# A reordered opening: inputs and square sums first, filter products in pairs, k/v blocks of one k-tile

## The chip, the cores and the metric

The kernel runs on one core of a Trainium2 chip (trn2). The metric is the device time of one execution in microseconds (us); lower is better. A profile of one execution lies beside the times. Engines: TensorE (PE; its weight loads are PEld), VectorE (DVE), ScalarE (ACT), GpSimd (POOL) and SyncE (SP, which issues nearly all transfers).

## The reference

One layer of a hybrid diffusion block, in float32, for 256 latent tokens `x` and 256 context tokens `ctx`, width 2048:

```python
mod = (silu(c) @ ada_w + ada_b)          # six vectors: sh1, sc1, g1, sh2, sc2, g2
mod_c = silu(c_ctx) @ ada_w + ada_b
h  = rmsnorm(x,   norm1_g) * (1 + sc1)  + sh1
hc = rmsnorm(ctx, norm1_g) * (1 + csc1) + csh1
q, k, v, f, hy = split(h @ w_in)
kc, vc = split(hc @ w_in[:, 1024:3072])
```

Behind it stand neighbourhood attention over the latent and all context keys (8 heads of 128), a 2-D Fourier mix of `f`, and a Hyena operator on `hy`: long convolutions through FFTs, whose filters are made by a small network of positions: `hdn = sin(freq * (z @ w1 + b1))`, `hdn = sin(freq * (hdn @ w2 + b2))`, `h = (hdn @ w3) * decay`. Each group has its own RMSNorm, then come `w_out`, a gated residual, a gated MLP with a depthwise convolution (11 x 512 hidden columns), another gated residual and a final RMSNorm.

## The kernel before

Activations lie transposed, features on the 128 partitions, 16 "k-tiles" of 128 features by 256 tokens. Large products are made in three passes of reduced-precision fp32 (fp32r): each operand is split into a rounded part `hi` and a remainder `lo`, and `mm3` (line 163) adds hi*hi, hi*lo and lo*hi. A weight chunk of 1 MB comes in two transfers of 512 KB into buffers called `raw` (8 of them, line 238), ACT casts it to `w_hi` (line 172) and DVE subtracts for `w_lo` (line 173); two chunks of split weights can exist. Small products are plain f32 matmuls, each of which the profile shows as two instructions.

**The k/v projection** (k and v of x and ctx together, 2048 columns) is the first large stage. Its 16 k-tiles are worked in `blocks=(2, 2, 4, 4, 4)`. A block has four groups (`group`, line 511): two for k (`kT`, 256-column matmuls) and two for v (`v_t`, 512-column matmuls). Each group fills four of the five `acc_ps` PSUM banks, and each block's sums go to `kT` and `v_t`: block 0 by a copy on ACT (line 534), later blocks by an add on DVE (line 536). Before a block can run, its k-tiles need the adaLN scale and shift: `prep_pieces` (line 439) loads the block's columns of `ada_w` (4 MB for two k-tiles), multiplies them with the two silu vectors (line 454, tiles of 32 columns, four side by side), transposes and reduces; then `hprep` (line 483) makes hi and lo of h and hc, per k-tile and input two DVE operations (lines 224, 229) and one on ACT (line 228). While block b runs, the pieces of block b+1 are made. `CFG["p1"]` says how many side steps (`pump`: two columns of adaLN rows for later stages, two DVE operations of line 317 and 1 MB of transfers) come in each block.

**The opening** comes before that. `CFG["start"]` lists its steps by short names: transfers (`hp`, `pk` the packed constants, `h3` hy_w3, `dc` decay, `ft` the DFT table, `x0 x1` and `c0 c1` the inputs, `a..` adaLN columns), `si` the silu, `n1s n2s` the two sine layers, `hw` sums of hy_w3, `w0` to `w3` warm-up matmuls whose results nobody reads, `fr` first filter rows, `f0 f1` the filters of the two orders, `s0 s1` their spectra, `q0 q1` square sums and `n0 n1` the norms of x and ctx, `p0 p1` adaLN of block 0, `w` the first weight chunks, `h0 h1` hi and lo of block 0, `e` a piece of block 1. The filters `kz` have one buffer, so `f0 s0 f1 s1` follow each other.

The order in the list is not the order on an engine. The framework that builds the program (Tile) orders each engine's queue itself, with the list as priorities and a table of expected costs, and sets all waits. Within a queue the chip then keeps that order.

**Square sums before:** ACT squares 512 columns at a time, DVE reduces four such into one [128, 256] part (line 427, eight in all), PE sums over partitions with one-column matmuls, DVE and ACT take the reciprocal root of two columns, and `rms_bcast` (line 201) spreads it again by two diagonal matrices (`dg`, line 212) and two matmuls:

```python
for t in range(2):
    dg = cst.tile([P, P], F32, tag="dg", name="dg", bufs=2)
    TS(dg[:], ident, r[:, t : t + 1], None, op0=ALU.mult)
    mm(ps[:, t * P : (t + 1) * P], ones[:], dg[:], True, True)
```

Of the kernel before, what the change touches and what calls it, by code (L numbers as in the profile page):

```python
# [8 lines left out]
F32 = mybir.dt.float32  # L9
# [26 lines left out]
for _n, _k in V_LAYOUT:  # L36
# [10 lines left out]
    p1=(3, 0, 3, 5, 6),  # L47
    blocks=(2, 2, 4, 4, 4),
# [78 lines left out]
def hybrid_block(ctx: ExitStack, tc: tile.TileContext, a: dict, out: bass.AP):  # L127
# [103 lines left out]
    class Weights:  # L231
        def __init__(self, stack, nraw, nsp, side=None):
            self.raw = pool(stack, "w_raw", nraw, side)
            self.sp = pool(stack, "w_split", nsp, side)

# [5 lines left out]
        def chunk(self, src, i, nk, n):  # L241
            raws = []
            for q in range(2):
                z = (slice(None), slice(q * nk // 2, (q + 1) * nk // 2))
                raws.append((z, self.load(src[2 * i + q], nk // 2, n)))
# [35 lines left out]
    class Pairs:  # L281
# [5 lines left out]
        def add(self):  # L287
            self.tiles.append(self.pool.tile([P, 2, L], self.dt, tag=self.pool.name, name=self.name, bufs=KT // 2))
# [68 lines left out]
    if True:  # L357
        hpack = w1.raw.tile([64, L + 2 * 64 + 3], F32, tag="raw", name="hpack")
        hw3, hwsd = spec[:64, 0], spec[:64, 1]
# [5 lines left out]
        hw2 = hpack[:, 67:131]  # L365
        zT = hpack[:33, 131 : 131 + L]
        hd1, hd2 = tb[:64, 2, :L], tb[:64, 2, L:]
# [5 lines left out]
        def sine(dst, w, src, b):  # L373
            ps = bank()
            mm(ps[:64, :L], w, src, True, True)
            arg, k = tb[:64, 3, :L], tb[:64, 3, L:]
            TS(arg, ps[:64, :L], hv[:, b : b + 1], hv[:, 2:3], op0=ALU.add, op1=ALU.mult)
# [5 lines left out]
            nc.scalar.activation(dst, arg, AF.Sin)  # L383
# [13 lines left out]
        def first_row(o):  # L397
            ps = bank()
            mm(ps[0:1, :], hd2[:, 0:1], hw3[:, 2 * o, :], True, True)
            TT(frow[:, o, :], ps[0:1, :], decay[0:1, 0, :], op=ALU.mult)  # L400

        def filters(o):
            for t in range(2):
                for z in range(2):
                    ps = bank()
                    mm(ps[:], hd2[:, t::2], hwsd[:, 2 * o + z, :], True, True)
                    TT(kz[:, 2 * z + t, :], ps[:], decay[:, t, :], op=ALU.mult)
            for z in range(2):
                nc.scalar.copy(kz[0:1, 2 * z, :], frow[:, o, :])
# [5 lines left out]
    if True:  # L415
# [4 lines left out]
        def squares(v):  # L420
            parts = []
            for q in range(4):
                pt = v_t[:, q, v * L : (v + 1) * L]
                sq = kT[:, 2 * (q % 2) : 2 * (q % 2) + 2, :].rearrange("p a (b n) -> p a b n", n=L)
                for j in range(2):
                    nc.scalar.activation(sq[:, j], xs[v].tiles[2 * q + j][:], AF.Square)
                nc.vector.tensor_reduce(pt, sq.rearrange("p a b n -> p n (a b)"), axis=AX.X, op=ALU.add)
# [55 lines left out]
        def hprep(k0, nk, vv):  # L483
            ts = []
            for k in range(k0, k0 + nk):
                hi, lo = hs[vv]
                A, B = (z[:, k, vv : vv + 1] for z in (A1, B1))
                ts.append((modulate(p1, xs[vv][:, k, :], A, rbs[vv][:]), B, hi[:, k, :]))
                if k % 2:
                    lo.add()  # L490
                    for i in range(2):
                        t, B, h = ts[i]
                        shift_split(t, B, h, lo[:, k - 1 + i, :])
                    ts = []
# [16 lines left out]
        def group(b, g):  # L511
# [19 lines left out]
            for u in range(4):  # L531
                dst = kT[:, 4 * g + u, :] if g < 2 else v_t[:, u, (g - 2) * 512 : (g - 1) * 512]
                if b == 0:
                    nc.scalar.copy(dst, pss[u][:])
                else:
                    TT(dst, pss[u][:], dst, op=ALU.add)
# [9 lines left out]
        def first_rows():  # L546
            first_row(0)
            first_row(1)

        def sq(v):  # L550
            parts[v] = squares(v)

        wn = CFG["warm"]
        steps = {
            "hp": lambda: nc.sync.dma_start(hpack[:], a["hpack"]),
            "pk": lambda: nc.sync.dma_start(pack[:], a["pack"]),
            "h3": lambda: nc.sync.dma_start(hw3, a["hy_w3"][0].rearrange("k (g n) -> k g n", n=HYW)),
# [4 lines left out]
            "w0": lambda: warm(ones[:], wn[0]), "w1": lambda: warm(decay[:, 0, :], wn[1]),  # L562
            "w2": lambda: warm(ftab.rearrange("p a n -> p (a n)"), wn[2]), "w3": lambda: warm(xs[0][:, 0, :], wn[3]),
# [3 lines left out]
            "a00": lambda: pre_ada(0, 0), "a01": lambda: pre_ada(0, 1), "a10": lambda: pre_ada(1, 0), "a11": lambda: pre_ada(1, 1),  # L567
# [5 lines left out]
        late = CFG["late"].split()  # L573
        for z in CFG["start"].split():
            steps[z]()
        for b in range(len(blocks)):
# [3 lines left out]
            for g in range(4):  # L580
# [3 lines left out]
                while late and b == 0:  # L584
                    z = late.pop(0)
                    if z == "|":
                        break
                    steps[z]()
# [322 lines left out]
def laid_out(inp):  # L911
# [25 lines left out]
    h = np.zeros((64, L + 2 * 64 + 3), f32)  # L937
    for i, n in enumerate(("hy_b1", "hy_b2", "hy_freq")):
        h[:, i] = inp[n][0]
    h[:33, 3:67] = inp["hy_w1"][0]  # L940
    h[:, 67:131] = inp["hy_w2"][0]
    h[:33, 131:] = z.T
# [4 lines left out]
    def tiled(chunks, halves=2):  # L947
        out = np.empty((len(chunks) * halves, P, 1024), f32)
        for i, (w, k, nk, c, n) in enumerate(chunks):
            nk //= halves  # L950
            for q in range(halves):
                z = inp[w][0, (k + q * nk) * P : (k + (q + 1) * nk) * P, c : c + n]
                out[halves * i + q] = z.reshape(nk, P, n).transpose(1, 0, 2).reshape(P, nk * n)
        return out
# [35 lines left out]
```

## Time and profile before

| | |
|---|---|
| median of 3 runs | 1358.14 us (1357.56 to 1358.69) |
| the profiled execution | 1356.83 us, its span 1354.8 us, granted TensorE clock 0.988 |
| PE busy | 1319.2 us, 97% of the span |
| DVE, ACT busy | 921.9 us (68%), 553.0 us (41%) |
| read from memory | 308 MB, 229 GB/s over the span |

"Busy" for PE means that some matmul was in the pipeline. In a group's row the name says what is written from what, then partitions x elements, count, busy us, mean ns of one, and the idle time of the engine just before with what ended it. A mean can be longer than the distance between two starts, since matmuls overlap. In the chain of waits each line is a start, a length and what the end of the program hung on then. The window rows give busy us (and counts) per engine, then the granted clock, the busy share of the transfer engines and their rate.

### The profile page before, as it was taken

The numbers are of one execution on the slowest core, as the hardware profiler recorded it, in microseconds if no ns is written. First come the engines' busy times: TensorE is split into PE (matmuls) and PEld (weight loads), VectorE is DVE, ScalarE is ACT, GpSimd is POOL, SyncE is SP. The second block draws the span as 40 slices with busy tenths as digits, with TensorE's granted clock in tenths as the row PEclk, the third lists the DMA queues.
The fourth block names the chain that finished last, engine by engine and source line by source line (L and its number), as shares of the span: only waits on it lengthen the run. The fifth ranks groups of instructions, "written<-read, shape, count | busy, mean of one in ns | idle before, by whom it ended". The sixth has DMA issues, their size and how long they took to land.

```text
span 1354.8 us, 24555 instructions
## 1 busy us (share of the span) xinstructions
PE 1319.2 (97%) x10318; PEld 1237.8 (91%) x10318; DVE 921.9 (68%) x1200; ACT 553.0 (41%) x741; POOL 43.6 (3%) x32
## 2 busy tenths in 40 slices
PE   8899999999989999999999999999999999999996
PEld 4587888899879889989999999999999999999996
DVE  5856658687999888976676767744445555554553
ACT  3443213143333665445444444433334444443442
POOL 0000000000422010000000000000000000000000
PEclk9899999999989999989999999999999999999998
DMA  8788678697776964846777777755555555555541
GB/s 320 264 313 332 256 287 315 239 345 237 215 264 234 349 208 158 288 147 205 259 252 251 240 250 252 269 188 189 186 187 189 184 188 190 187 187 189 185 152 62
DMA packets 92894, 311.96 MB, mean 230 GB/s; under 512 B 15984, under 2 KB 16176, under 8 KB 92464
## 3 DMA queue, kind: packets, MB, share of 16 engines
q1 hardware_dynamic: 92784, 310.41, 66.4%
q8 instruction: 80, 1.31, 0.4%
q14 instruction: 30, 0.25, 0.0%
HBM read 308.27 MB, written 2.10 MB: 229 GB/s over the span
## 4 chain that ended last, share of the span: by engine, by line
PE 89%; DVE 6%; issue 2%; ACT 1%; DMA 1%; POOL 0%; DVEq 0%; ACTq 0%; POOLq 0%
PE acc_ps L161 82%; PE mi_ps L161 4%; PE mi_ps L454 2%; DVE w_lo L173 2%; DVE acc L317 1%; PE mi_ps L169 1%; DMA raw<-in_ada_t 1%; DMA raw<-in_ada_col_t 0%; DVE X L736 0%; DVE xr L906 0%; DVE u L654 0%; ACT w_hi L172 0%; DVE u L746 0%; DVE u L655 0%; DVE Y L729 0%
## 5 line engine op out<-in xcount | busy, mean ns | idle before, releaser
L173 DVE TENSOR_TENSOR w_lo<-raw,w_hi 128x1024 fp32r<-128x1024 f32 x376 | 453.5, 1236 | 234.7 <-ACT w_hi L172 233.4
L172 ACT CAST w_hi<-raw 128x1024 fp32r<-128x1024 f32 x376 | 380.3, 1048 | 515.3 <-PE acc_ps L161 452.0
L161 PE MATMUL acc_ps<-h_hi,w_hi 128*128 128x256 f32 x1408 | 395.5, 281 | 1.6 <-ACT h_hi L228 1.6
L161 PE MATMUL acc_ps<-h_hi,w_lo 128*128 128x256 f32 x1408 | 395.4, 281 | 0.0
L161 PE MATMUL acc_ps<-h_lo,w_hi 128*128 128x256 f32 x1408 | 395.4, 281 | 0.0
L161 PEld LDWEIGHTS acc_ps<-h_hi,w_hi 128*128 128x128 f32 x1408 | 266.1, 189 | 1.8 <-ACT h_hi L228 1.8
L161 PEld LDWEIGHTS acc_ps<-h_lo,w_hi 128*128 128x128 f32 x1408 | 266.1, 189 | 0.0
L161 PEld LDWEIGHTS acc_ps<-h_hi,w_lo 128*128 128x128 f32 x1408 | 266.1, 189 | 0.0
L161 PE MATMUL acc_ps<-yh,w_lo 128*128 128x256 f32 x704 | 197.1, 280 | 0.0
L161 PE MATMUL acc_ps<-yl,w_hi 128*128 128x256 f32 x704 | 197.1, 280 | 0.0
L161 PE MATMUL acc_ps<-yh,w_hi 128*128 128x256 f32 x704 | 196.8, 280 | 0.0
L317 DVE SCALAR_TENSOR_TENSOR acc<-raw,s_t,acc 128x1024 f32<-128x1024 f32 x120 | 160.6, 1338 | 32.6 <-DMA raw<-in_ada_col_t 31.8
L161 PE MATMUL acc_ps<-hx_hi,w_lo 128*128 128x256 f32 x512 | 146.1, 286 | 4.9 <-DVE w_lo L173 4.9
L161 PE MATMUL acc_ps<-hx_hi,w_hi 128*128 128x256 f32 x512 | 146.4, 286 | 0.0
L161 PE MATMUL acc_ps<-hx_lo,w_hi 128*128 128x256 f32 x512 | 145.0, 283 | 0.0
L161 PEld LDWEIGHTS acc_ps<-yl,w_hi 128*128 128x128 f32 x704 | 132.4, 188 | 0.0
L161 PEld LDWEIGHTS acc_ps<-yh,w_hi 128*128 128x128 f32 x704 | 132.2, 188 | 0.0
L161 PEld LDWEIGHTS acc_ps<-yh,w_lo 128*128 128x128 f32 x704 | 132.1, 188 | 0.0
L161 PEld LDWEIGHTS acc_ps<-hx_hi,w_lo 128*128 128x128 f32 x512 | 97.5, 191 | 7.6 <-DVE w_lo L173 5.5
L161 PEld LDWEIGHTS acc_ps<-hx_hi,w_hi 128*128 128x128 f32 x512 | 97.7, 191 | 4.3 <-issue 4.2
L161 PEld LDWEIGHTS acc_ps<-hx_lo,w_hi 128*128 128x128 f32 x512 | 97.6, 191 | 0.5 <-issue 0.4
L633 DVE SCALAR_TENSOR_TENSOR xr<-acc_ps,G,xr 128x256 f32<-128x256 f32 x64 | 26.9, 477 | 25.1 <-PE acc_ps L161 25.1
(225 smaller groups left out, 1595.2 us busy)
## 6 DMA issues: line engine op xcount, KB each, us to landing
raw<-in_ffn_t SPq DMA_DIRECT2D x264, 512.0 KB, 4.2
raw<-in_ada_col_t SPq DMA_DIRECT2D x128, 512.0 KB, 5.0
raw<-in_ada_t SPq DMA_DIRECT2D x64, 512.0 KB, 6.4
raw<-in_w_in_t SPq DMA_DIRECT2D x48, 512.0 KB, 5.6
raw<-in_w_kv_t SPq DMA_DIRECT2D x32, 512.0 KB, 5.2
raw<-in_w_out_t SPq DMA_DIRECT2D x32, 512.0 KB, 4.8
x_in<-in_xT SPq DMA_DIRECT2D x8, 256.0 KB, 7.3
x_in<-in_cT SPq DMA_DIRECT2D x8, 256.0 KB, 8.2
```

Of the source, the lines that this page charges most:

```text
L161: nc.tensor.matmul(ps, lhsT, rhs, start=start, stop=stop, skip_group_check=True)
L169: nc.tensor.transpose(ps, src, ident[:n, :n])
L172: nc.scalar.copy(hi, src)
L173: TT(lo, src, hi.bitcast(F32), op=ALU.subtract)
L317: STT(acc[:], r[:, 0, :], sc, acc[:], op0=ALU.mult, op1=ALU.add)
L454: nc.tensor.matmul(ps[32 * j : 32 * j + 32, :w], s_t[:, kt, :], raws[kt // (n2 // 2)][:, kt % (n2 // 2), :], start=kt < 4, stop=kt >= KT - ...
L633: STT(xr[:, c, :], pss[nt // 2][:, (nt % 2) * L : (nt % 2 + 1) * L], cols[:, c : c + 1], xr[:, c, :], op0=ALU.mult, op1=ALU.add)
```

## The change

1. **Order.** The list becomes the one in the diff. The two packs are issued from ACT, and SP starts with x and ctx, then hy_w3, decay, the DFT table, the adaLN columns of block 0 and, early, the first weight chunk (`W`). Warm-up: 8 matmuls on ones and 3 on `pack`; the 11 others go.
2. **Square sums.** PE multiplies the squared tiles with a matrix of ones, 16 matmuls of 256 columns per input, which leaves the sum on all partitions; `rms_rows` takes the reciprocal root on [128, 256] and no broadcast is needed.
3. **Filter products.** hy_w3 and hy_w2 are held twice, on partitions 0 to 63 and 64 to 127, so that two products of 64 rows lie on the two halves of the array and are issued next to each other into two banks.
4. **Blocks.** `blocks` becomes (1, 1, 2, 4, 4, 4), `p1` (0, 2, 1, 3, 5, 6). A chunk of one k-tile has 2048 columns and comes in two column halves; the host lays it out so. Block 0's v copies go to DVE. `hprep` makes one k-tile at a time, and the pool of pairs for `lo` gets one buffer more.

```diff
-    p1=(3, 0, 3, 5, 6),
-    blocks=(2, 2, 4, 4, 4),
+    p1=(0, 2, 1, 3, 5, 6),
+    blocks=(1, 1, 2, 4, 4, 4),
...
-    start='hp pk h3 dc ft x0 x1 si w0 n1s w1 n2s hw w2 w3 a00 a01 a10 fr q0 f0 p0 a11 p1 n0 h0 s0 c0 w c1 f1 e s1 q1 n1 h1 e',
-    late='',
-    warm=(8, 2, 6, 3),
+    start='hp pk x0 x1 c0 c1 h3 dc ft a0 a1 W wm si n1s wp n2s q0 q1 n0 hw n1 fr f0 s0 f1 p0 p1 w h0 h1 s1 e',
+    warm=(8, 3),
...
+    def rms_rows(pool_, ps, n, name):
+        ms = pool_.tile([P, L], F32, name=f"{name}_m", tag="rr_m")
+        TS(ms[:], ps[:, :L], 1.0 / n, EPS, op0=ALU.mult, op1=ALU.add)
+        s = pool_.tile([P, L], F32, name=f"{name}_s", tag="rr_s")
+        r = pool_.tile([P, L], F32, name=f"{name}_r", tag=f"{name}_r")
+        nc.scalar.activation(s[:], ms[:], AF.Sqrt)
+        nc.vector.reciprocal(r[:], s[:])
+        STT(s[:], r[:], -0.5, ms[:], op0=ALU.mult, op1=ALU.mult)
+        TT(s[:], s[:], r[:], op=ALU.mult)
+        STT(r[:], s[:], 1.5, r[:], op0=ALU.add, op1=ALU.mult)
+        return r
...
+                if nk > 1:
+                    z = (slice(None), slice(q * nk // 2, (q + 1) * nk // 2))
+                    raws.append((z, self.load(src[2 * i + q], nk // 2, n)))
+                else:
+                    z = (slice(None), slice(None), slice(q * n // 2, (q + 1) * n // 2))
+                    raws.append((z, self.load(src[2 * i + q], 1, n // 2)))
+            return raws
+
+        def load_early(self, src, i, nk, n):
+            self.early[id(src), i] = self.loads(src, i, nk, n)
...
-        hpack = w1.raw.tile([64, L + 2 * 64 + 3], F32, tag="raw", name="hpack")
-        hw3, hwsd = spec[:64, 0], spec[:64, 1]
+        hpack = w1.raw.tile([P, L + 3 * 64 + 3], F32, tag="raw", name="hpack")
+        hw3, hwsd = spec[:, 0], spec[:, 1]
...
+        def rows(o):
+            return slice(64 * o, 64 * o + 64)
...
         def filters(o):
             for t in range(2):
+                pss = [bank(acc_ps) for _ in range(2)]
                 for z in range(2):
-                    ps = bank()
-                    mm(ps[:], hd2[:, t::2], hwsd[:, 2 * o + z, :], True, True)
-                    TT(kz[:, 2 * z + t, :], ps[:], decay[:, t, :], op=ALU.mult)
+                    mm(pss[z][:], hd2[rows(z), t::2], hwsd[rows(z), 2 * o + z, :], True, True)
+                for z in range(2):
+                    TT(kz[:, 2 * z + t, :], pss[z][:], decay[:, t, :], op=ALU.mult)
...
         def squares(v):
-            parts = []
-            for q in range(4):
-                pt = v_t[:, q, v * L : (v + 1) * L]
-                sq = kT[:, 2 * (q % 2) : 2 * (q % 2) + 2, :].rearrange("p a (b n) -> p a b n", n=L)
-                for j in range(2):
-                    nc.scalar.activation(sq[:, j], xs[v].tiles[2 * q + j][:], AF.Square)
-                nc.vector.tensor_reduce(pt, sq.rearrange("p a b n -> p n (a b)"), axis=AX.X, op=ALU.add)
-                parts.append(pt)
-            return parts
-
-        def normalise(v, parts):
-            rbs[v] = rms_bcast(p1, parts, D, f"rs{v}")
+            ps = bank(acc_ps)
+            for q in range(KT // 2):
+                sq = kT[:, (q + 4 * v) % NH, :].rearrange("p (k n) -> p k n", n=L)
+                nc.scalar.activation(sq, xs[v].tiles[q][:], AF.Square)
+                for i in range(2):
+                    mm(ps[:, :L], ones[:], sq[:, i], q + i == 0, q == KT // 2 - 1 and i == 1)
+            return ps
+
+        def normalise(v, ps):
+            rbs[v] = rms_rows(p1, ps, D, f"rs{v}")
...
-                if b == 0:
+                if b == 0 and g < 2:
                     nc.scalar.copy(dst, pss[u][:])
+                elif b == 0:
+                    nc.vector.tensor_copy(dst, pss[u][:])
                 else:
                     TT(dst, pss[u][:], dst, op=ALU.add)
...
+        def load_w3():
+            for z in range(2):
+                nc.sync.dma_start(hw3[64 * z : 64 * z + 64], a["hy_w3"][0].rearrange("k (g n) -> k g n", n=HYW))
...
-            "hp": lambda: nc.sync.dma_start(hpack[:], a["hpack"]),
-            "pk": lambda: nc.sync.dma_start(pack[:], a["pack"]),
+            "hp": lambda: nc.scalar.dma_start(hpack[:], a["hpack"]),
+            "pk": lambda: nc.scalar.dma_start(pack[:], a["pack"]),
```

More of the change, by code (lines that the diff above doesn't have):

```diff
@@ L234, in __init__ @@
             self.sp = pool(stack, "w_split", nsp, side)
+            self.early = {}
         def load(self, src, nk, n):
@@ L364, in hybrid_block @@
         hw1 = hpack[:33, 3:67]
-        hw2 = hpack[:, 67:131]
-        zT = hpack[:33, 131 : 131 + L]
-        hd1, hd2 = tb[:64, 2, :L], tb[:64, 2, L:]
+        hw2 = hpack[:64, 67:195]
+        zT = hpack[:33, 195 : 195 + L]
+        hd1, hd2 = tb[:64, 2, :L], tb[:, 2, L:]
         def silu():
@@ L487, in hprep @@
                 A, B = (z[:, k, vv : vv + 1] for z in (A1, B1))
-                ts.append((modulate(p1, xs[vv][:, k, :], A, rbs[vv][:]), B, hi[:, k, :]))
-                if k % 2:
+                t = modulate(p1, xs[vv][:, k, :], A, rbs[vv][:])
+                if k % 2 == 0:
                     lo.add()
[L491 to L494, printed above, removed]
+                shift_split(t, B, hi[:, k, :], lo[:, k, :])
         w_specs, w_at = [], {}
@@ L561, in hybrid_block @@
             "si": silu, "n1s": lambda: sine(hd1, hw1, zT, 0), "n2s": lambda: sine(hd2, hw2, hd1, 1), "hw": sums,
-            "w0": lambda: warm(ones[:], wn[0]), "w1": lambda: warm(decay[:, 0, :], wn[1]),
-            "w2": lambda: warm(ftab.rearrange("p a n -> p (a n)"), wn[2]), "w3": lambda: warm(xs[0][:, 0, :], wn[3]),
+            "wm": lambda: warm(ones[:], wn[0]), "wp": lambda: warm(pack[:, :384], wn[1]), "W": lambda: w1.load_early(*w_specs[0]),
             "c0": lambda: load_pairs(xs[1], a["cT"], 0), "c1": lambda: load_pairs(xs[1], a["cT"], 1),
@@ L572, in hybrid_block @@
         }
-        late = CFG["late"].split()
         for z in CFG["start"].split():
@@ L583, in hybrid_block @@
                 group(b, g)
[L584 to L588, printed above, removed]
                 budget += CFG["p1"][b] / 4.0
```

48 lines of the change are left out of this document (24 added, 24 removed).

## The prediction

> **What bounds the kernel now.** I read the page first, then a table of the opening stretches, then the chain of waits, then the groups of the opening, keeping shapes apart. The page and its chain:
>
> ```profile
> span 1354.8 us, 24555 instructions
> PE 89%; DVE 6%; issue 2%; ACT 1%; DMA 1%; POOL 0%; DVEq 0%; ACTq 0%; POOLq 0%
> ```
>
> TensorE (PE) sets the time. Where does it not? The table by stretch (busy us of PE, PEld, DVE, ACT, POOL; then granted clock, DMA share, GB/s):
>
> ```profile
> 0.00:27.00 27.00, 22.11 (x54) 10.80 (x54) 18.09 (x27) 8.40 (x15) 0.90 (x7) 1.00 0.93 332
> 27.00:40.00 13.00, 6.96 (x87) 4.61 (x87) 6.87 (x20) 7.16 (x11) 0.00 (x0) 0.86 0.88 328
> 40.00:48.00 8.00, 7.66 (x18) 3.35 (x17) 7.96 (x13) 4.90 (x9) 0.00 (x0) 0.79 0.90 327
> 48.00:65.40 17.40, 17.25 (x135) 10.77 (x134) 14.78 (x30) 4.25 (x9) 0.00 (x0) 1.00 0.50 169
> 65.40:114.00 48.60, 48.59 (x323) 37.59 (x323) 28.78 (x55) 21.25 (x36) 0.00 (x0) 1.00 0.87 335
> 114.00:230.00 116.00, 116.00 (x760) 94.01 (x760) 79.01 (x126) 27.73 (x38) 0.00 (x0) 1.00 0.78 289
> ```
>
> From 65.4 to 230 us PE is never idle (48.59 of 48.60, 116 of 116), while VectorE (DVE) works 59% and 68% of it. So the k/v projection is pure PE time, and whatever the change wins, it wins before 65.4 us. The chain there (start, us, what), and then the issues of the two inputs from SyncE (SP):
>
> ```profile
> 27.21 1.91 PE mi_ps L454 x32
> 31.66 7.45 DMA raw<-in_ada_t
> 39.11 0.29 DVE dg L212
> 62.42 0.44 DVE rs_b L215
> 65.41 18.77 PE acc_ps L161 x109
> 84.17 3.57 PE mi_ps L454 x32
> 89.19 10.77 PE acc_ps L161 x90
> ```
>
> ```profile
> 3.65 6.84 SPq L352 DMA_DIRECT2D x_in<-in_xT  x8
> 16.86 4.16 SPq L352 DMA_DIRECT2D x_in<-in_cT  x4
> 29.65 1.91 SPq L352 DMA_DIRECT2D x_in<-in_cT  x4
> ```
>
> The second half of the context is issued only at 29.65 us, behind weight loads that wait for a buffer; its norm's broadcast ends at 62.86 us (rs_b), and the half of group 0 that needs it waits as long. The groups up to 65.4 us, PE's and then DVE's (busy us, mean ns, idle before):
>
> ```profile
> L161 PE MATMUL mi_ps<-kz,ftab 128*128 128x512 f32 x16 | 8.6, 688 | 0.0
> L161 PE MATMUL mi_ps<-spec,v_t 64*128 64x512 f32 x16 | 8.0, 617 | 0.3 <-ACT kz L180 0.3
> L454 PE MATMUL mi_ps<-raw,s_t 128*32 128x256 f32 x128 | 7.9, 383 | 0.0
> L161 PE MATMUL acc_ps<-hx_hi,w_hi 128*128 128x256 f32 x10 | 3.0, 301 | 0.0
> L161 PE MATMUL mi_ps<-spec,v_t 64*1 64x512 f32 x4 | 1.9, 588 | 0.0
> L161 PE MATMUL mi_ps<-dg,ones 128*128 128x128 f32 x8 | 1.9, 373 | 5.0 <-DVE dg L212 5.0
> L169 PE MATMUL mi_ps<-pack,adasb 128*128 128x128 f32 x8 | 1.7, 292 | 1.0 <-ACT adasb L456 1.0
> L161 PE MATMUL mi_ps<-v_t,hpack 64*64 64x256 f32 x2 | 1.1, 657 | 3.9 <-ACT v_t L383 3.9
> L161 PE MATMUL acc_ps<-hc_hi,w_hi 128*128 128x256 f32 x5 | 0.9, 302 | 0.0
> ```
>
> ```profile
> L427 DVE TENSOR_REDUCE v_t<-kT 128x256 f32<-128x1024 f32 x8 | 15.3, 1927 | 0.0
> L407 DVE TENSOR_TENSOR kz<-mi_ps,v_t 128x512 f32<-128x512 f32 x8 | 5.3, 691 | 2.1 <-PE mi_ps L161 2.1
> L173 DVE TENSOR_TENSOR w_lo<-raw,w_hi 128x1024 fp32r<-128x1024 f32 x4 | 4.9, 1220 | 0.0
> L224 DVE SCALAR_TENSOR_TENSOR ht<-x_in,A,rs_b 128x256 f32<-128x256 f32 x4 | 1.8, 480 | 0.0
> L193 DVE RECIPROCAL rs_r<-rs_s 128x2 f32<-128x2 f32 x2 | 0.3, 161 | 0.3 <-ACT rs_s L192 0.3
> ```
>
> In the opening DVE is in the way: its eight square reductions cost 15.3 us and PE waits 5.0 us for a diagonal (dg) queued behind them.
>
> **The yardstick.** PE is the bound from some point on, so I compare one number: the time at which PE would have started the k/v stream had all other opening work up to the adaLN of the first four k-tiles been done before. Before: by 65.41 us three products of 10 matmuls on hx and five on hc are done, some 35 of the stream's; 90 matmuls in 10.77 us make 0.12 us each, so 4.2 us. Yardstick 65.4 - 4.2 = **61.2 us**.
>
> **The change part by part.** In the new order PE first does the sine products as now, with the second one near 9.7 to 10.8 us (the 3.9 us wait for ACT in its row stays; three warm-up matmuls on pack fill it). From 10.8 us PE owes the following.
>
> Squares on PE: 2 inputs x 16 matmuls, two instructions each, 64 in all. Nearest row, same shape:
>
> ```profile
> L161 PE MATMUL acc_ps<-x_in x6: 379/380/380, 20.3 to 21.4; 128*128 128x256 f32 x6
> ```
>
> Six starts over 1.1 us, 0.22 us each: **14.1 us**. It removes the 15.3 us of DVE reductions and, on PE, the one-column products and the diagonals. The context's squares queue PE behind its landing, but not for long: four instructions per 512 columns are 0.88 us, and ACT feeds them faster:
>
> ```profile
> L426 ACT ACTIVATE kT<-x_in 128x512 f32<-128x512 f32 x16 | 9.5, 625 | 2.7 <-DVE v_t L427 1.4 <-DMA x_in<-in_xT 1.2
> ```
>
> Filter products: 16 instructions of 512 columns, and 4 for the first rows. Their pace in full clock is visible in the weight loads of the same width:
>
> ```profile
> 15.18 0.34 PEld L161 LDWEIGHTS acc_ps<-ftab 128*128 128x128 f32 x1 [0.52 <-issue]
> 16.02 0.19 PEld L161 LDWEIGHTS acc_ps<-ftab 128*128 128x128 f32 x1 [0.51 <-issue]
> 16.45 0.19 PEld L161 LDWEIGHTS acc_ps<-ftab 128*128 128x128 f32 x1 [0.24 <-issue]
> ```
>
> 0.43 us from 16.02 on, so alone 6.9 + 1.7 = 8.6 us. Now two at a time lie on rows 0 to 63 and 64 to 127. Do such pairs overlap? No row pair is in the trace, but column strips are: the L454 products run 32 instructions of 256 columns in 1.91 us, 0.06 each, where one such alone takes 0.22. So bounds 4.3 (full overlap) and 8.6; I take **4.3**, because strips demonstrably overlap nearly fourfold. Spectra, unchanged: 16 x 0.43 = **6.9**.
>
> AdaLN: the blocks (2, 2) become (1, 1, 2). A part of 256 columns costs 1.91, of 512 columns 3.57; the step between is 1.66, so half of it below 1.91 gives 1.1 for 128 columns, and no saving would give 1.91. I take 1.45. Four parts of 1.45 and two of 1.91 make **9.6**, against 7.9 before. Transposes, 8 at 0.22: **1.8**.
>
> Sum 14.1 + 4.3 + 6.9 + 9.6 + 1.8 = 36.7, from 10.8: yardstick 47.5 if PE has no gap, **13.7 us earlier** than 61.2. What is taken from that:
>
> Clock: in the rows above, a 512-column instruction takes 0.84 us until 16.02 and 0.43 after, although PE was busy from 1 us on and off. If the same holds, 5.2 us of the squares run at half pace and lose 2.6. The added warm-up may bring full pace at once, 0. I take **1.3**. The Trainium skill, "TensorE: Matmul & The Clock Gate", section "Part 1: The HAM clock gate", has the clock freed after about 3.4 us of sustained work in a free-running window; by that the new order would be at full pace near 10 us and this term 0.
>
> Transfers: the first 27 us moved 332 GB/s x 27 = 9.0 MB. The new order wants 9.7 MB before the first weights are whole (x and ctx 4.2, hy_w3 twice 1.05, tables and packs 1.3, adaLN 2.1, weights 1.05), near 29 us at 0.4 MB/us; the first weight half is there near 27.5, and usable at 30 after a cast and a subtraction of 1.22 (L173 above):
>
> ```profile
> L172 ACT CAST w_hi<-raw 128x1024 fp32r<-128x1024 f32 x376 | 380.3, 1048 | 515.3 <-PE acc_ps L161 452.0
> ```
>
> PE has work to 36 by then, so this costs **0**; without that work it would cost 3 to 4 us. The two packs move to ACT's queue, idle until the first one lands. hy_w3 now stands behind both inputs and lands when 5.75 MB are through, near 18 us (5.75 / 0.332 = 17.3); DVE's hy sums wait for it, and behind them in its queue the filters, which need the same data anyway. The context passes SP's queue ahead of every wait for a buffer; hp, four adaLN and two weight pieces fill 7 of 8 buffers.
>
> Waits: kz is one buffer, so filters, spectra, filters, spectra remain a chain. A spectrum is 8 x 0.43 and two sums of 0.69 (L407's price), 4.8 us; filling kz is four products of 0.69 and the copies behind them, some 3.6 (an estimate). From 21 us, when decay is there, the chain ends near 21 + 2 x 8.4 = 38; other PE work lies between. Norms: Sqrt and five DVE steps on 128x256. I take 0.48 as for the 128x256 product of L224 also for the reciprocal (0.16 for two columns is the lower bound, a doubled 0.96 the upper), some 2.2 us per input. PE gaps of 0 to 5 us; I take **2.2**. The skill's "VectorE: DVE Perf Modes", section "First, the fixed hardware budget", has reciprocal as an iterative divide with eight repeats; as an estimate from it 256 columns take 2.1 us and the two norms 3.3 us more of DVE. No run here shows it; it would bring 1351 to some 1353.
>
> DVE in the small blocks, the one real danger. Each block after the first adds 16 accumulator banks onto k and v:
>
> ```profile
> L536 DVE TENSOR_TENSOR kT<-acc_ps,kT 128x512 f32<-128x512 f32 x24 | 16.2, 688 | 15.8 <-PE acc_ps L161 15.7
> L317 DVE SCALAR_TENSOR_TENSOR acc<-raw,s_t,acc 128x1024 f32<-128x1024 f32 x19 | 24.3, 1280 | 0.1
> ```
>
> That is 11.0 us per block, now twice within four k-tiles instead of once, and block 0 gives DVE its 8 value copies too (8 x 0.69 = 5.5). From the landing of hy_w3 near 18 us: opening 24.9 (22 operations of 512 columns at 0.69: 15.2; norms 4.4; first split 2.4; modulation, 4 x 0.48: 1.9; small ones 1.0), block 0 10.8 (5.5 + 2.4 + 1.9 + 1.0), block 1 25.8 (16 sums 11.0, four half splits 4.9, modulation 3.8, two side steps of two L317 each 5.1, small 1.0), block 2 about 25 (11.0, one split 2.4, modulation 7.7, one side step 2.6, small 1.0). Together 86.5, so DVE could be through at 104.5 us. PE: 47.5 + 4 x 11.4 (48 matmuls of 0.12 and 24 of double width) + 3.57 x 2 + 1.8 = 102, plus 3.5 above. The two loads are equal, and block 1 alone is 25.8 us of DVE against 16.2 of PE (11.4, two adaLN parts of 1.91, transposes). With five accumulator banks and groups of four, PE can run ahead by one bank only. Lower bound 0 (the last bank sums and a side step slip into block 2), upper 9.6 (25.8 - 16.2); I take **3**, because the sums over all blocks are equal and only their order can cost.
>
> Total: 13.7 - 1.3 - 2.2 - 3 = **7.2 us**. The profiled execution took 1356.8 us, 2.0 outside its span of 1354.8; less 7.2, 1349.6. The median of the three runs shown lies 1.3 above the profiled one, 1358.1, so I forecast **1350.9**. After block 2 nothing changes: 17 side steps are spread over the blocks as before (0+2+1+3+5+6 against 3+0+3+5+6), and PE stays the bound.
>
> **Rivals.** A difference under 0.2% (2.7 us) can't be told from none.
>
> Gapless: DVE keeps up, pairs overlap, clock free early. Speaks for it: DVE's 59% after 65.4. Against: the equal loads above. Gain 10 to 13.7, about 1346. Chance 0.16.
>
> DVE paces blocks 1 and 2: 6 to 9.6 us lost there instead of 3, gain 0.6 to 4.2, about 1355.5. For it: 25.8 against 16.2. Chance 0.18, two thirds of it over the 2.7 us.
>
> Transfers pace it: by 114 us the kernel had moved 9.0 + 4.3 + 2.6 + 2.9 + 16.3 = 35 MB. The new one needs this by about 106; at 0.4 MB/us after 27 us there is room for 40. Only if buffer waits idle the queue for 12 us (as 17.4 us at 169 GB/s did, because nobody freed buffers) is the gain eaten: about 1358, the change then only moves the wait. Chance 0.09.
>
> Slower: bank sums are queued on DVE behind splits, modulation and side steps instead of ahead of them. PE then waits for each group's four sums, 2.75 us x 8 groups = 22 us in blocks 1 and 2, and the sum is 22 - 13.7 = +8, 1366. It decides from 13.7 of the 22 exposed. Against it: before, sums at the same place waited for PE (15.8 us idle before them), not the other way round. Chance 0.09.
>
> **The numbers.** Forecast 0.48, its own range 1347.5 to 1354 (terms 0.5 to 4 better or worse). Faster: 0.48 + 0.16 + 0.12 = 0.76; same: 0.06 + 0.07 = 0.13; slower: 0.09 + 0.02 = 0.11. Range 1345.5 to 1359: it leaves out the best end of the gapless case and the slower one.
>
> **What would show it.** Right: ctx issued before 10 us; squares' matmuls at 0.22 us from about 10 to 25; filter pairs near 0.22 per instruction; first k/v matmul at 34 to 40 us and PE without gaps from there to 114 but for 2 to 4 us at DVE's bank sums; DVE over 90% busy from 40 to 100. Wrong: filter instructions still 0.43 apart (4.3 us), a stretch at half clock after 25 us (up to 3.4 of 6.8 us), PE waiting for adaLN transfers, or bank sums standing behind L317 on DVE.

## The result and the profile after

The changed kernel takes 1365.86 us in the median (1364.15 to 1368.48, 4 runs), the kernel before 1357.94 us beside it (1357.56 to 1358.69). The ratio is 1.0054, with a 95% interval from 1.0034 to 1.0074: about 8 us slower, where 7.2 us faster was forecast. The profiled execution took 1366.53 us, 9.7 more than that of before, and its span is 9.8 us longer. Two executions are left out of the medians and ratios below, one of x8 (2609.91 us) and one of the kernel before beside it (4113.94 us), because they took about two and three times as long as all others. From the page of the changed kernel, the span, the engines and the chain:

```profile
span 1364.6 us, 24705 instructions
PE 1331.4 (98%) x10390; PEld 1240.4 (91%) x10390; DVE 926.0 (68%) x1218; ACT 548.7 (40%) x736; POOL 45.4 (3%) x32
PE 89%; DVE 6%; ACT 2%; issue 2%; DMA 1%; POOL 0%; DVEq 0%; ACTq 0%; POOLq 0%; SPq 0%
```

PE is busy for 12.2 us more than before (1319.2), so the loss is not idle time. It is work, or work that takes longer. The table by stretch, columns as in the prediction:

```profile
0.00:27.00 27.00, 23.97 (x101) 18.43 (x103) 11.49 (x25) 14.18 (x25) 0.90 (x7) 1.00 0.96 308
27.00:40.00 13.00, 9.98 (x18) 3.53 (x14) 8.14 (x14) 3.39 (x6) 0.00 (x0) 0.74 0.53 208
40.00:48.00 8.00, 7.17 (x77) 3.58 (x76) 7.48 (x17) 5.49 (x9) 0.00 (x0) 1.00 0.60 218
48.00:65.40 17.40, 16.88 (x176) 13.59 (x176) 14.58 (x32) 8.52 (x17) 0.00 (x0) 1.00 0.79 299
65.40:114.00 48.60, 48.60 (x310) 31.94 (x310) 32.03 (x64) 8.05 (x13) 0.00 (x0) 1.00 0.88 334
114.00:230.00 116.00, 116.00 (x716) 85.94 (x715) 77.59 (x128) 27.85 (x42) 0.00 (x0) 1.00 0.77 279
```

Two things are to be seen. From 27 to 40 us PE is idle for 3.0 us, its clock is 0.74 and the transfers run at 208 GB/s, where the kernel before moved 328. And from 65.4 to 230 us PE is never idle, yet it issues 716 matmuls from 114 to 230 us where the kernel before issued 760 in the same time: 6% fewer from an equally busy engine.

The lead can be followed by the time at which each kernel has done the projection up to a given k-tile. The work of the second k-tile starts at 64.7 us instead of 72.8 (the kernel before works two k-tiles at once, and 72.8 us is when half of its first block is done), the fifth at 116.7 instead of 120.0, the ninth at 181.8 instead of 175.6, and the attention stage at 462.1 instead of 452.6. The lead is there early and is lost between 100 and 230 us; the 9.5 us at the attention stage stay to the end (9.8).

The groups of the adaLN products on PE from 55 to 260 us, before and then after (mean ns of one, then idle before):

```profile
L454 PE MATMUL mi_ps<-raw,s_t 128*32 128x512 f32 x192 | 24.5, 596 | 0.0
L454 PE MATMUL mi_ps<-raw,s_t 128*32 128x256 f32 x32 | 1.9, 382 | 0.0
```

```profile
L482 PE MATMUL mi_ps<-raw,s_t 128*32 128x512 f32 x192 | 37.4, 601 | 0.0
L482 PE MATMUL mi_ps<-raw,s_t 128*32 128x256 f32 x64 | 3.9, 382 | 0.0
```

The same 192 instructions of 512 columns, with the same duration of one (596 and 601 ns), keep PE busy for 12.9 us more. So the single instruction is not slower; they overlap less. The chain shows why. First three pieces of before, then the changed kernel's from 77 us on:

```profile
112.57 1.83 PE mi_ps L454 x10
117.42 2.69 PE mi_ps L454 x18
120.54 0.98 PE mi_ps L454 x4
```

```profile
77.43 1.83 PE mi_ps L482 x10
79.26 0.89 PE acc_ps L160 x3
80.15 0.99 PE mi_ps L482 x6
81.14 1.72 PE acc_ps L160 x10
82.86 0.98 PE mi_ps L482 x4
83.84 0.91 PE acc_ps L160 x6
84.75 0.98 PE mi_ps L482 x4
85.74 1.73 PE acc_ps L160 x13
87.47 0.98 PE mi_ps L482 x4
```

A product is two instructions, and k-tile `kt` lies on strip `kt % 4` (line 481). Sixteen products in a row, x32, take 3.57 us: four rounds of four strips, 0.89 a round. A transfer of a four-k-tile block brings two k-tiles, so a piece x4 is the two products of one transfer: two strips work, two stand empty, and it costs a whole round of 0.98. Eight such pieces are 7.8 us instead of 3.57. In the changed kernel's program, the framework's planner puts weight matmuls of the k/v stream between them; in the program of before it left the sixteen mostly together. In the chains from 60 to 260 us the 192 instructions stand in 29 pieces after and in 8 before, which makes 37 rounds instead of 26. A switch of the array between two tilings could be a price of its own, but there is little room for it: a round alone costs 0.97 to 0.99 us and a round in a row 0.89, so the 21 further pieces add some 2 us, the 11 further rounds some 10.

The 256-column products are no loss. In the changed kernel two of their parts fall behind 55 us, before it was one; with the parts of 128 columns (4.3 us) the changed kernel has 8.2 us of them in all, the kernel before 7.9.

### The profile page after: what moved, and what is told of

Read it like the earlier page. It is cut to its first block, busy times and chain, and to the rows that moved or that the text cites. A ratio compares the mean times of both kernels' runs of the same rounds, so it can differ in the third digit from the quotient of the medians.

```text
span 1364.6 us, 24705 instructions
## 1 busy us (share of the span) xinstructions
PE 1331.4 (98%) x10390; PEld 1240.4 (91%) x10390; DVE 926.0 (68%) x1218; ACT 548.7 (40%) x736; POOL 45.4 (3%) x32
## 4 chain that ended last, share of the span: by engine, by line
PE 89%; DVE 6%; ACT 2%; issue 2%; DMA 1%; POOL 0%; DVEq 0%; ACTq 0%; POOLq 0%; SPq 0%
PE acc_ps L160 81%; PE mi_ps L160 3%; PE mi_ps L482 3%; DVE w_lo L172 2%; PE mi_ps L168 1%; DVE acc L340 1%; DMA raw<-in_ada_col_t 1%; DMA pack<-in_pack 0%; ACT kT L454 0%; DVE Y L748 0%; DVE X L755 0%; DVE xr L925 0%; DVE rs_r L223 0%; ACT w_hi L171 0%; DVE u L765 0%
## 5 line engine op out<-in xcount | busy, mean ns | idle before, releaser
L160 PEld LDWEIGHTS acc_ps<-hx_hi,w_lo 128*128 128x128 f32 x512 | 97.1, 190 | 10.2 <-DVE w_lo L172 5.5
L484 ACT COPY adasb<-mi_ps 128x512 f32<-128x512 f32 (+2 forms) x12 | 5.3, 444 | 105.2 <-PE mi_ps L482 105.1
```

The lines of the kernel that those rows point to most:

```text
L160: nc.tensor.matmul(ps, lhsT, rhs, start=start, stop=stop, skip_group_check=True)
L484: nc.scalar.copy(sb[:, :w], ps[:, :w])
```

## The experiments

The theory (A in what follows): the split products cost the time. The rivals: the short first blocks do, by their own work; the new opening does; DVE's load in the short blocks does, and the pairs are only its sign. In the expectations below, A is always the split products. B is DVE's bank sums or the small blocks themselves, C an opening that is late. D has two meanings: late transfers in x7 and x8, DVE's load in x9 and x10.

The table gives, for all kernels, the adaLN products' busy time from 55 to 260 us, the start of the attention stage in the profiled execution, the median and the ratio to before with its interval. The first column holds the 512-column products and what smaller ones fall behind 55 us, 1.9 us before, 3.9 in the changed kernel, 5.6 in x3. From the attention stage to the end the profiled executions take 904 to 909 us, so the second column and the times agree to some 4 us only.

| kernel | products, us | attention at, us | median, us | ratio |
|---|---|---|---|---|
| before | 26.4 | 452.6 | 1357.94 (1357.80 to 1358.94 beside the experiments) | 1 |
| changed | 41.3 | 462.1 | 1365.86 | 1.0054 (1.0034 to 1.0074) |
| x1: changed, column halves | 31.0 | 450.1 | 1356.31 | 0.9978 (0.9966 to 0.9989) |
| x2: new opening, old blocks | 40.5 | 462.3 | 1370.73 | 1.0087 (1.0058 to 1.0115) |
| x3: old opening, new blocks | 36.8 | 466.0 | 1373.42 | 1.0098 (1.0069 to 1.0127) |
| x4: changed, last transfer first | 25.7 | 457.6 | 1366.41 | 1.0055 (1.0037 to 1.0072) |
| x5: before, column halves | 24.9 | 453.5 | 1360.32 | 1.0010 (0.9997 to 1.0023) |
| x6: x2, column halves | 30.6 | 453.2 | 1359.82 | 1.0010 (0.9997 to 1.0023) |
| x7: changed, adaLN ahead of filters | 40.4 | 460.6 | 1367.65 | 1.0068 (1.0047 to 1.0090) |
| x8: x7, column halves | 30.8 | 451.3 | 1355.95 | 0.9992 (0.9982 to 1.0001) |
| x9: changed, side steps late | 29.4 | 448.3 | 1353.40 | 0.9958 (0.9943 to 0.9973) |
| x10: changed, pieces late | 31.6 | 452.2 | 1357.69 | 0.9989 (0.9972 to 1.0005) |
| x11: x9, filters ahead of norms | 30.0 | 442.7 | 1346.78 | 0.9910 (0.9896 to 0.9925) |
| x12: x11, products ahead of spectrum | 29.2 | 441.8 | 1349.81 | 0.9934 (0.9916 to 0.9952) |

### x1: all four strips from one transfer

```diff
+                nf = nk // 2 if nk == 4 else 1
+                wf, sf = w // nf, 4 // nf
                 for kt in range(KT):
-                    j = kt % 4
-                    nc.tensor.matmul(ps[32 * j : 32 * j + 32, :w], s_t[:, kt, :], ...)
+                    for f in range(nf):
+                        j = kt % sf * nf + f
+                        nc.tensor.matmul(ps[32 * j : 32 * j + 32, :wf], s_t[:, kt, :], ...)
...
```

Each product of 512 columns becomes two of 256 on two strips, so the two k-tiles of a transfer fill all four, and it no longer matters whether they stand alone. The copies, transposes and reductions behind them follow the new layout, with half as many transposes.

> The changed kernel with one edit: in the adaLN products of a block of four k-tiles, the 512 columns of a k-tile are taken as two halves of 256, each on its own 32-column strip, so that the two k-tiles that one transfer brings fill all four strips. Theory A (the adaLN products are now issued in pairs, 0.98 us for a pair instead of 0.45 within a run of sixteen; 39.1 us after 60 us instead of 23.9): products after 60 us fall to 24 to 28 us and the time by 8 to 12 us, to 1354 to 1358. Theory B (DVE's bank sums in the small blocks hold PE up): products get shorter but PE waits instead, time 1363 to 1367. Theory C (the opening itself is late): same as B.

Its group, from 55 to 260 us:

```profile
L485 PE MATMUL mi_ps<-raw,s_t 128*32 128x256 f32 x448 | 31.0, 386 | 0.0
```

31.0 us instead of 41.3, and the median falls by 9.5 us, the attention stage begins 12 us earlier. The two go together as A has it. The products miss A's 24 to 28 us: they still stand in 29 pieces. The time, 1356.31, is in A's range and 0.2% under before.

### x2, x3, x6: opening and blocks apart

x2 is the changed kernel with the old `blocks` and `p1`, x3 the kernel before with the new ones (and with the loads and the `hprep` that they need); x6 is x2 with the column halves of x1. The edit of x2, where the list of steps also gets one more transfer step (`a01`) for block 0's columns; that of x3 is the reverse:

```diff
-    p1=(0, 2, 1, 3, 5, 6),
-    blocks=(1, 1, 2, 4, 4, 4),
+    p1=(3, 0, 3, 5, 6),
+    blocks=(2, 2, 4, 4, 4),
```

> The new opening with the old blocks (2, 2, 4, 4, 4) and side steps (3, 0, 3, 5, 6); the adaLN columns of block 0 come as before in eight transfers. Theory A: the products are split here too (the first four of the four-k-tile parts almost wholly into pairs), about 13 us lost, 1360 to 1367. Theory B (the small blocks cost it): 1350 to 1355. Theory C: 1364 or more.

> The kernel before with the new blocks (1, 1, 2, 4, 4, 4) and side steps only; the opening, the square sums and the filters stay as before. Theory A: some products are split in the order that this kernel gets, about 5 us more than before, and 1.3 us more of products: 1361 to 1365. Theory B: 1364 to 1368. Theory C: 1357 to 1360.

> The new opening with the old blocks (x2) and the column halves. Theory A: about 10 to 12 us less than x2, 1357 to 1361, which is the new opening without the pairs. Rival (what x2 lost is not the pairs): over 1364.

The groups of x2 and of x3:

```profile
L482 PE MATMUL mi_ps<-raw,s_t 128*32 128x512 f32 x192 | 36.9, 601 | 0.1
```

```profile
L462 PE MATMUL mi_ps<-raw,s_t 128*32 128x512 f32 x192 | 31.2, 599 | 0.0
```

Either half of the change alone is slower than before, and in both the products are split. So it isn't the short blocks, whose work x2 doesn't have; it is an order that tips with either part. With the halves x2 comes back from 462.3 to 453.2 at the attention stage, and x6's time is in A's range. x2 and x3 are both slower than A's ranges (1360 to 1367 and 1361 to 1365). In x3 the 512-column products cost 6.7 us more than before and the smaller ones of the first 260 us 1.8 more (9.7 for 7.9), of the 13.4 us that it is late at the attention stage. The other 5 are not taken apart; in the trace of x3 PE has waits of 2.0 us from 55 us on (0.2 before) and a granted clock of 0.82 from 27 to 65.4 us (0.91 before).

### x5: the same remedy where nothing is split

x5 is the kernel before with the edit of x1 in its `prep_pieces`.

> The kernel before with the column halves of x1 only. It splits two of its six large adaLN products, which cost 5.5 and 4.1 us instead of 3.57. Theory A: it gains what these splits cost and half the transposes, 2 to 3.5 us. Rival (the halves are worth more than the splits, for instance by fewer switches of the array's tiling): 5 us or more. If it gains nothing, what x1 won is not the pairs.

No gain: A and the rival both miss. By the expectation's last sentence this would speak against the pairs. But x5 had little of their cost to take away: the products were nearly whole already (24.9 us for 26.4), and PE then waits 2.6 us ahead of the transposes for ACT's copy, which about fits the 0.9 us by which its attention stage starts later. So x5 neither shows A nor ends it; x9 and x10, which have no halves, have to decide. By the traces the halves are worth something only where the pairs stand alone; the new opening (x6 for x5) brings 0.3 us at the attention stage, the new blocks (x1 for x6) 3.1.

### x4: whole pieces by waiting for the last transfer

```diff
-                for kt in range(KT):
+                for z in range(KT):
+                    kt = KT - 1 - z
...
```

The last transfer's k-tiles come first, so that none of the products can start before all have landed.

> The changed kernel with the k-tiles of each adaLN product taken from the last transferred to the first, so that a product starts when all its data is there and runs in one piece of sixteen. Theory A: six products of 3.57 us, 21.4 instead of 35.3 us; against that PE may wait for whole sets of eight buffers. Time 1352 to 1362, products without a gap. Theory B: 1363 to 1368. Theory C: as B.

Its groups from 55 to 260 us, then two stretches:

```profile
L483 PE MATMUL mi_ps<-raw,s_t 128*32 128x512 f32 x192 | 21.8, 595 | 0.7 <-DMA raw<-in_ada_t 0.7
L168 PE MATMUL mi_ps<-pack,adasb 128*128 128x128 f32 x28 | 4.7, 284 | 5.9 <-ACT adasb L485 5.9
```

```profile
65.40:114.00 48.60, 44.46 (x314) 32.79 (x312) 32.76 (x64) 7.15 (x11) 0.00 (x0) 1.00 0.74 286
114.00:230.00 116.00, 108.40 (x719) 87.41 (x720) 74.06 (x127) 28.90 (x44) 0.00 (x0) 0.99 0.77 295
```

The products cost 15.6 us less, and PE is idle for 11.7 us in these stretches (4.1 and 7.6) where the changed kernel had no idle time. Half of it, 5.9 us, is the transposes' wait for ACT's copy of the finished sums; w_hi, ACT's cast of the weights, takes 2.2, the rest of ACT and DVE 2.7 and the transfers themselves 0.9. How much of this goes back to buffers that are held until all eight transfers are there isn't shown. The attention stage starts 4.5 us earlier than in the changed kernel, but the median is the same: A's range is missed, and the time lies where B and C had it. That the loss is idle time and not longer products keeps A alive, no more. Wholeness forced in this way exchanges one cost for another.

### x9, x10: whole pieces by moving other work

x9 takes the side steps out of the first three blocks, x10 leaves them and asks for the pieces one group of tokens later.

```diff
-    p1=(0, 2, 1, 3, 5, 6),
+    p1=(0, 0, 0, 4, 6, 7),
```

```diff
-                while todo and n0 - len(todo) < n0 * (g + 1) / 4:
+                while todo and n0 - len(todo) < n0 * g / 4 + (b < 2):
```

> The changed kernel with its side steps (the multiply-adds of column 8) taken out of blocks 1 and 2: 0, 0, 0, 4, 6, 7 per block instead of 0, 2, 1, 3, 5, 6, the same 17 in all. Nothing is left out. In the program's order nearly all adaLN products now stand in whole pieces (eight of 16 products, one 16, one 14, and a few small ones) instead of in pairs. Theory A (the pairs cost the time): the adaLN products after 55 us, 37.4 us of PE in the changed kernel, fall to 25 to 28, the attention stage starts 9 to 11 us earlier, time 1354 to 1357. Rival D (VectorE is what is late in blocks 1 and 2, the pairs being only its sign): the time falls about as much here, so this run alone does not tell; the run with late pieces and unchanged side steps does. If neither: 1364 to 1367.

> The changed kernel with the side steps as they are (0, 2, 1, 3, 5, 6), but the planner is asked for the next k-tiles' preparation one group of tokens later in blocks 0 and 1. Nothing is left out. In the program's order six adaLN pieces of 16 products stand first, then x10, three x2, x10, two x2, then four of 16. VectorE has just as much to do in blocks 1 and 2 as in the changed kernel. Theory A (pairs): products after 55 us cost 27 to 31 us instead of 37.4 and the time is 1355 to 1359. Rival D (VectorE's load in blocks 1 and 2): products may be whole, but TensorE then waits for VectorE by as much, time 1363 to 1367.

The groups of x9 and of x10:

```profile
L482 PE MATMUL mi_ps<-raw,s_t 128*32 128x512 f32 x192 | 25.5, 597 | 0.0
```

```profile
L482 PE MATMUL mi_ps<-raw,s_t 128*32 128x512 f32 x192 | 27.7, 597 | 0.4 <-DMA raw<-in_ada_t 0.4
```

Both as A expects in the products, by two edits that have only the order in common; the 512-column products stand in 10 pieces in x9 and 12 in x10. In time x10 is as expected, and x9 goes past it (13.8 us earlier at the attention stage for 9 to 11). x10 keeps DVE's work in the short blocks (its side steps, line 340, take 3.8 us of DVE from 65.4 to 114 us, as in the changed kernel, and none in x9) and still comes back by 8 us. So D falls, but for 1.3 us that PE waits for DVE's sums in x10. About 1 us of x10's gain is not the order's: its first k/v matmul is at 48.8 us instead of 50.05, behind the same opening at a higher granted clock (0.81 from 31 to 40 us instead of 0.62). x9 is the better one: 0.42% faster than before. Its chain has a price list of pieces, all of which are one round of strips, but for the third:

```profile
105.99 0.97 PE mi_ps L482 x2
108.56 0.99 PE mi_ps L482 x8
112.56 2.69 PE mi_ps L482 x18
115.56 0.98 PE mi_ps L482 x4
```

One product (x2), two (x4) and four (x8) take the same 0.97 to 0.99 us, nine (x18) take three rounds.

### x7, x8, x11, x12: what kept the opening from its forecast

The first k/v matmul starts at 50.05 us, not at 34 to 40. DVE's queue of the changed kernel, then PE's and SP's (start, us, engine):

```profile
21.16 1.75 DVE L223 RECIPROCAL rs_r<-rs_s 128x256 f32<-128x256 f32 x1 [3.40 <-ACT rs_s L222]
24.59 2.48 DVE L417 TENSOR_TENSOR spec<-spec 128x512 f32<-128x512 f32 x4
26.99 1.75 DVE L223 RECIPROCAL rs_r<-rs_s 128x256 f32<-128x256 f32 x1
30.46 0.67 DVE L437 TENSOR_TENSOR kz<-acc_ps,v_t 128x512 f32<-128x512 f32 x1
```

```profile
31.18 3.01 PE L160 MATMUL acc_ps<-spec,v_t 64*128 64x512 f32 x4 [3.02 <-DVE kz L437]
34.12 6.08 PE L160 MATMUL mi_ps<-kz,ftab 128*128 128x512 f32 x8
41.19 1.08 PE L482 MATMUL mi_ps<-raw,s_t 128*32 128x128 f32 x32
```

```profile
25.64 0.33 SPq L613 DMA_DIRECT2D gtab<-in_dft_g  x1
41.89 7.27 SPq L250 DMA_DIRECT2D raw<-in_ada_t  x8
```

A chain of delays. The second reciprocal stands ahead of the filters' sums; PE waits 3.0 us for kz; after the wait its clock is halved, so eight spectrum instructions take 6.08 us instead of 3.60 (the second spectrum's); the products of the first k-tile stand behind the spectrum and hold their buffers, so SP, at the next buffer, issues nothing from 25.97 to 41.89 us. x7 puts adaLN and the first norm's consumers ahead of hy_w3 and the filters, x8 adds the halves:

```diff
-  hp pk x0 x1 c0 c1 h3 dc ft a0 a1 W wm si n1s wp n2s q0 q1 n0 hw n1 fr f0 s0 f1 p0 p1 w h0 h1 s1 e
+  hp pk x0 x1 c0 c1 a0 a1 W h3 dc ft wm si n1s wp n2s q0 q1 n0 p0 p1 n1 h0 h1 w hw fr f0 s0 f1 s1 e
```

> The changed kernel with another order of the opening: SP brings the adaLN columns and first weights before hy_w3, decay and table, and the adaLN products of block 0 come directly after the square sums, so that their four buffers are free near 27 instead of 42 us; modulation comes before the weight split. The products of the later blocks are split in its order as in the changed kernel. Theory A (the order's splits cost it, however early the data): products after 55 us stay at 35 us or more, and only the earlier start of the stream counts, 3 to 6 us: 1360 to 1363. Theory D (late transfers behind full buffers cost it, and the splits are harmless): 1352 to 1357.

> x7 with the column halves. Theory A: both gains add up, 9 to 10 us less than x7: 1350 to 1354. Theory D: as x7.

x7's first k/v matmul is at 44.1 us, 6 us earlier, and its products stay at 40.4 us as A has it, but the time is no better and outside A's range and D's: hy_w3 now comes late, PE waits 1.4 us for it, the clock from 27 to 40 us falls to 0.61, and the second spectrum is still to be done inside the stream. x8 comes back by nearly 12 us, a little more than A's 9 to 10, but from x7's higher time: it ends above A's 1350 to 1354 and is no faster than before. x11 keeps the transfers' order and changes only the steps, with x9's `p1`:

```diff
-  ... q0 q1 n0 hw n1 fr f0 s0 f1 p0 p1 w h0 h1 s1 e
+  ... q0 hw q1 fr f0 n0 n1 s0 p0 p1 f1 h0 h1 w s1 e
```

x12 has `fr f0 p0 p1 n0 n1 s0 f1` there.

> The run with late side steps, and in the opening the filters' sums and tables stand before both norms' reciprocals on VectorE, the adaLN transfer of the first k-tile behind them, hp and the first k-tiles before the last weight pieces. Nothing is left out. If the late reciprocal and the late filter sums are what kept the opening from its forecast: the fill of kz starts 3 to 4 us earlier than 31 us, the first k/v matmul starts at 45 to 48 us instead of 50, and the attention stage 2 to 4 us earlier than in the run with late side steps: 1351 to 1354. If the opening is set by other things (the transfers, the half clock): no more than 1 us from that run.

> As the run with the filters before the norms, but the adaLN products of the first two k-tiles stand ahead of the first spectrum on TensorE. Nothing is left out. If TensorE's waits for kz are filled by them: 1 to 3 us better than that run, 1349 to 1353, and no half clock from 31 to 40 us. If it only exchanges one wait for another: within 1 us of it.

DVE, PE and SP of x11:

```profile
25.43 2.49 DVE L417 TENSOR_TENSOR spec<-spec 128x512 f32<-128x512 f32 x4
29.03 2.46 DVE L437 TENSOR_TENSOR kz<-acc_ps,v_t 128x512 f32<-128x512 f32 x4
31.42 1.73 DVE L223 RECIPROCAL rs_r<-rs_s 128x256 f32<-128x256 f32 x1
```

```profile
29.76 1.13 PE L160 MATMUL acc_ps<-spec,v_t 64*128 64x512 f32 x2 [0.75 <-DVE kz L437]
30.95 3.70 PE L160 MATMUL mi_ps<-kz,ftab 128*128 128x512 f32 x8
34.58 1.08 PE L482 MATMUL mi_ps<-raw,s_t 128*32 128x128 f32 x32
43.85 0.38 PE L160 MATMUL acc_ps<-hx_hi,w_hi 128*128 128x256 f32 x1
```

```profile
35.29 9.06 SPq L250 DMA_DIRECT2D raw<-in_ada_t  x8
```

On DVE the difference up to there is the second reciprocal with the three short steps that follow it, now behind the filters, and every link is gone (the times are against the changed kernel's): a wait of 0.75 us, no half clock, the products of the first k-tile 6.6 us earlier, SP's next issue 6.6 us earlier, the first k/v matmul at 43.85 us. The fill of kz comes 2.2 us earlier than in x9 (31.26 us there), less than the 3 to 4 expected, and the attention stage 5.6 us earlier, more than the 2 to 4: the rest is what the wait had set off. At 1346.78 us x11 beats both kernels: 0.9% under before, some 19 us under the changed one. x12 was expected 1 to 3 us better still and isn't, though it has no half clock from 31 to 40 us either: its first k/v matmul is at 37.9 us, but PE waits 1.1 us for kz inside the stream and the second k-tile starts at 59.4 us for x11's 58.6. Its attention stage starts 0.9 us earlier than x11's, its median is 3 us higher, and the intervals of the two ratios just overlap: no gain over x11 is shown.

## Why the prediction was wrong

**The step that failed** is "After block 2 nothing changes". Its working counted the side steps, which stayed 17, and took the products of the later blocks as they stood before. They cost 37.4 us instead of 24.5. The first two parts stood in the prediction's own sum for PE, as "3.57 x 2", on the way to the fifth k-tile; in the chain of the changed kernel they take 12.5 us. The price was in the trace of before: 0.98 us for x4 in the chain, beside 3.57 for x32. The prediction's own argument that strips "demonstrably overlap nearly fourfold" was used for the filters and not turned round: four strips in a round are worth four only if four stand next to each other in the queue, and a new `blocks`, `p1` and opening give the planner another order. The Trainium skill, "TensorE: Matmul & The Clock Gate", section "Measured speedup vs the span model", gives a pack of tiles the duration of one matmul and some 4 ns for each further tile; by that a pack of two costs what a pack of four does, and the rows agree (0.98 for x4, 0.99 for x8).

**The yardstick** went from 61.2 us to about 55.6 (the second k-tile starts at 64.7 us; less 11.4 for the first, plus 2.3 for a part of block 2 and its transposes that were still to come), a lead of 5.6 us where the terms before DVE's gave 13.7 - 1.3 - 2.2 = 10.2. With the splits mended, but that opening, x1 gains 2.6 us of the 7.2 forecast. The terms, one by one:

- Squares 14.1: right. Their group in the opening of the changed kernel, 64 matmuls and 14.2 us:

```profile
L160 PE MATMUL acc_ps<-kT,ones 128*128 128x256 f32 x64 | 14.2, 381 | 0.0
```

- Filter pairs 4.3: mis-sized. Where the pairs stand next to each other they overlap as the strips do, the four first-row instructions in 1.0 us and ten in 2.85, nearer the lower bound than 0.43 each. But four come behind the wait and take 2.9 at the halved clock, and the last product, two instructions, stands alone and takes 1.1. Together 7.9 us, nearer the upper bound of 8.6.
- AdaLN, 1.45 for a part of 128 columns: it was 1.08. This term was too high by 1.5 in four parts.
- Reciprocal 0.48: mis-sized, and its upper bound of 0.96 too. It takes 1.75 us (L223 above), nearer the 2.1 that stood there as an estimate from the Trainium skill, "VectorE: DVE Perf Modes", section "First, the fixed hardware budget". The two make 2.5 us more of DVE, in front of the filters.
- Clock 1.3, at the squares: wrong place. The granted clock is 1.00 up to 27 us; the half clock came behind the wait at 31 us, as the prediction's list of signs had it, and took 2.5 us of the spectrum alone.
- Waits 2.2: PE was idle for 3.0 us from 27 to 40 us, and for 1.4 more from 40 to 65.4. The term was too low by half, and what the wait set off was not in it.
- DVE in the small blocks, 3: not seen as a wait. PE has no gap between 65.4 and 230 us, and x10 has the same DVE load without the loss.

**The rivals.** Gapless: it fell with these 4.4 us of idle time and the half clock. The transfers: SP did stand still, for 16 us, but PE never waited for it later; the loss isn't there. The slower case had 1366, the measured time, by another mechanism: no bank sum kept PE waiting. That the number fits says nothing for it. All rivals and the forecast priced the time from 114 us on as unchanged, and none could be right.

**Open** are why the planner's order tips (the runs show what tips it, not by which of its expected costs), some 5 us of x3, and some 2 of the 15 us that the stream lost against a lead of 5.6 us, of which the products explain 12.9. (From 230 to 420 us the changed kernel's PE is idle for 7.8 us, the kernel before for 6.9; that may be one of the two.)

## What to carry to other kernels

Where several small matmuls share the array, price the round and not the instruction, and ask for each group what stands next to it in the queue: here 192 unchanged instructions took 12.9 us more because a planner interleaved them in twos. When a change moves priorities or block sizes and the order is made by a program, compare the order of the whole stage after it, not only of the edited part; what isn't edited can still be reordered. And an engine that is fully busy can be losing time: count its instructions per stretch beside its busy share.

## What was not expected of the hardware

- One, two and four 32-column products of 512 columns take the same 0.97, 0.98 and 0.99 us when they stand alone (x9).
- A wait of PE of 3.02 us was followed by a half clock (0.62 over 31 to 40 us), one of 0.75 us in x11 was not. But the longest wait is not the whole of it: in x7 the granted clock is 0.50 from 30 to 36 us, behind waits of at most 0.71 us, four of them from 25 to 31 us; and in x2, x4 and x10 the same wait of 3.02 us left 0.81 over 31 to 40 us. The stretch in the changed kernel, then in x11:

```profile
31.00:40.00 9.00, 8.81 (x12) 3.19 (x12) 4.14 (x8) 3.39 (x6) 0.00 (x0) 0.62 0.30 118
```

```profile
31.00:40.00 9.00, 8.91 (x80) 4.32 (x81) 8.96 (x20) 5.96 (x10) 0.00 (x0) 1.00 0.65 232
```

- A reciprocal of 128x256 takes 1.75 us on DVE, four times a product of that size (0.42).
